# Average pooling over a contiguous input: the completion wait of two output stores moved behind the closing barriers, and the results moved from pool tiles to fixed SBUF tensors

## The chip, the cores and the metric

The kernel runs on one core of one Trainium2 chip. The metric is the device time of one execution in microseconds; the time before is the median of three runs. Beside these runs one execution was recorded by the hardware profiler; its rows are what the prediction works from. Engine names are those of the profile: DVE is VectorE, ACT is ScalarE, POOL is GpSimd, SP is SyncE, PE is TensorE. A "q" behind a name (SPq, POOLq) means the engine's sequencer, which issues DMAs and executes waits and barriers.

## What is computed

The input `x` has the shape (32, 256, 4096) in float32, 134.22 MB; `output_size` is 256. Each of the 32 x 256 = 8192 rows is cut into 256 windows of 16 neighbouring values, and the output (32, 256, 256) holds the mean of each window, 8.39 MB:

```python
for i in range(output_size):
    start = int(i * length / output_size)
    end = int((i + 1) * length / output_size)
    result[:, :, i] = np.mean(x[:, :, start:end], axis=-1)
```

## The kernel before

The 8192 rows are worked on in 16 tiles of 128 partitions x 4 rows: one tile is 128 x 16384 float32 values, 8.39 MB. The first fifteen tiles belong to one view of the input in which each partition owns 60 neighbouring rows (`x_many`), the last tile to a second view with 4 rows a partition (`x_last`). The one loop runs over the tiles `t`. In each turn

- SP issues the load of the tile into a buffer of `inpool` (L66). The pool has two buffers of 64 KiB a partition, so the load of tile t+2 waits until both reductions of tile t are done. In the last turn SP then issues the store of all fifteen earlier results, `o_many` from `res_many` (L68), in one DMA of 7.86 MB.
- POOL adds, for the second half of the tile's windows, the upper eight values of each window onto the lower eight, in place (L69).
- DVE sums the windows of the first half, sixteen values each (L74), and then those of the second half, eight values each (L77).
- ACT multiplies the tile's 1024 sums a partition by 1/16, in place (L80).

Behind the loop SP issues the second store, `o_last` from `res_last` (L85), 0.52 MB. Both stores wait for ACT. All DMAs of the kernel go through SP's one queue, in program order: sixteen loads, the large store, the small store.

The results lie in two tiles of a pool with one buffer each, `res_many` (60 KiB a partition) and `res_last` (4 KiB). The tile framework gives out the addresses and every semaphore. In bytes from the start of a partition, the two input buffers begin at 16,640 and 82,176 and the results at 147,712 and 209,152; a small tile `pad` that nothing reads or writes lies ahead of them and has the effect that all of them begin at a multiple of 256.

What follows the kernel's last instruction is written by the framework when its context closes; in the profile it carries the line of the `with` statement, L116. It is, in this order:

1. on SP, four waits for the eight DMA semaphores that loads and stores share (the third has the semaphore of the small store, the fourth that of the large one), then a drain that waits for ACT;
2. a barrier over all five engines: each reports to POOL, and POOL releases them;
3. on POOL, a drain and one instruction that clears the framework's semaphores, and a drain;
4. a second barrier of the same kind.

After that the runtime's own closing code runs, a barrier over the engines and the reset of all semaphores; it lies outside the profile's span.

Of the kernel before, what the change touches and what calls it, by code (L numbers as in the profile page):

```python
# [1 line left out]

# [4 lines left out]


@with_exitstack
def kernel(  # L10
    ctx: ExitStack,
    tc: tile.TileContext,
    x: bass.AP,
    output_size: int,
    out: bass.AP,
):

    nc = tc.nc
    F32 = mybir.dt.float32
    X = mybir.AxisListType.X

    batch, channels, length = x.shape
    ob, oc, olen = out.shape
    assert ob == batch and oc == channels and olen == output_size
    assert length % output_size == 0
    window = length // output_size  # L30
    hw = window // 2
    inv_w = 1.0 / float(window)

    P = nc.NUM_PARTITIONS
    R = 4
    rows = batch * channels
    assert rows % (P * R) == 0
    ntiles = rows // (P * R)
    many = (ntiles - 1) * R
    cells = R * output_size  # L40
    m = cells // 2
    cols = R * length

    xr = x.rearrange("b c l -> (b c) l")
    orow = out.rearrange("b c o -> (b c) o")
    x_many = xr[0 : P * many, :].rearrange("(p r) l -> p (r l)", p=P, r=many)
    o_many = orow[0 : P * many, :].rearrange("(p r) o -> p (r o)", p=P, r=many)
    x_last = xr[P * many :, :].rearrange("(p r) l -> p (r l)", p=P, r=R)
    o_last = orow[P * many :, :].rearrange("(p r) o -> p (r o)", p=P, r=R)

    padpool = ctx.enter_context(tc.tile_pool(name="padpool", bufs=1))
    padpool.tile([P, 32], F32, name="pad")
    inpool = ctx.enter_context(tc.tile_pool(name="inpool", bufs=2))
    respool = ctx.enter_context(tc.tile_pool(name="respool", bufs=1))
    res_many = respool.tile([P, (ntiles - 1) * cells], F32, name="res_many")
    res_last = respool.tile([P, cells], F32, name="res_last")

    for t in range(ntiles):
        last = t == ntiles - 1
        xin = inpool.tile([P, cells, window], F32, name="xin")  # L60
        if last:
            res, base, src = res_last, 0, x_last
        else:
            res, base = res_many, t * cells
            src = x_many[:, t * cols : (t + 1) * cols]
        nc.sync.dma_start(out=xin.rearrange("p o w -> p (o w)"), in_=src)  # L66
        if last:
            nc.sync.dma_start(out=o_many, in_=res_many[:, :])  # L68
        nc.gpsimd.tensor_add(  # L69
            out=xin[:, m:cells, 0:hw],  # L70
            in0=xin[:, m:cells, 0:hw],
            in1=xin[:, m:cells, hw:window],
        )
        nc.vector.reduce_sum(  # L74
            out=res[:, base : base + m], in_=xin[:, 0:m, :], axis=X
        )
        nc.vector.reduce_sum(  # L77
            out=res[:, base + m : base + cells], in_=xin[:, m:cells, 0:hw], axis=X
        )
        nc.scalar.mul(  # L80
            out=res[:, base : base + cells],
            in_=res[:, base : base + cells],
            mul=inv_w,
        )
    nc.sync.dma_start(out=o_last, in_=res_last[:, :])  # L85


# [1 line left out]
_INS = ['x', 'output_size']  # L89
_OUTS = [((32, 256, 256), 'float32')]  # L90

_NUMBERS = {'output_size': 256}


# [26 lines left out]
```

## Time and profile before

| | |
|---|---|
| median of 3 runs | 334.69 us (334.52 to 334.81) |
| the profiled execution | 335.07 us |
| its span, first to last instruction | 333.3 us |
| DMA engines, share of the span | 99.1 % (142.61 MB, 428 GB/s) |
| DVE busy | 209.7 us (63 %) |
| POOL busy | 139.7 us (42 %) |
| ACT busy | 18.2 us (5 %) |

The span runs from the first to the last instruction of the program; the profiled execution took 1.8 us more than its span. A busy share is an average over the whole span. Where times inside the span are given below, they count from its start. The trace also keeps each sequencer instruction and each update of a semaphore with its own time; where the text gives a time to the nanosecond it comes from there.

### The profile page before, as it was taken

To read this page: it belongs to the slowest core of one execution; us is meant where nothing else is said; L and a number is where in the kernel's file an instruction comes from. 1 tells how busy PE (TensorE), PEld (TensorE's weight loads), DVE (VectorE), ACT (ScalarE), POOL (GpSimd) and SP (SyncE) were. 2 spreads that over 40 slices of the span, in tenths; PEclk is the share of its full clock that TensorE was granted. 3 is DMA by queue.
4 is the path that set the end of the run, shared out by engine and by line. 5 is a ranking of instruction groups with operands and counts; after the bars stand their busy time and mean duration, and the time that the engine had idled before them with its cause. 6 is when DMAs were issued, how large, how long until landed. Compare 5 with 4: busy or idle time off the path is not lost.

```text
span 333.3 us, 158 instructions
## 1 busy us (share of the span) xinstructions
DVE 209.7 (63%) x32; ACT 18.2 (5%) x17; POOL 139.7 (42%) x20
## 2 busy tenths in 40 slices
DVE  0039295693929568392957849294774929487491
ACT  1000101000010100001010100101010010101001
POOL 0027090643709063360907346090724519082460
DMA  9898989999898989899898989899998989898996
GB/s 378 378 503 378 503 378 472 409 401 480 378 503 378 503 378 496 385 433 448 385 496 378 503 378 503 378 472 409 401 480 378 503 378 503 378 496 385 391 442 299
DMA packets 2592, 142.61 MB, mean 428 GB/s; under 512 B 288, under 2 KB 288, under 8 KB 416
## 3 DMA queue, kind: packets, MB, share of 16 engines
q1 hardware_dynamic: 2592, 142.61, 99.1%
HBM read 134.22 MB, written 8.39 MB: 428 GB/s over the span
## 4 chain that ended last, share of the span: by engine, by line
DMA 66%; POOL 18%; DVE 11%; POOLq 3%; issue 0%; ACT 0%; SPq 0%
DMA xin<-in_x_dram 66%; POOL xin L69 18%; DVE res_many L77 9%; POOLq L116 3%; DVE res_last L77 1%; ACT res_last L80 0%; SPq L66 0%; POOLq L69 0%
## 5 line engine op out<-in xcount | busy, mean ns | idle before, releaser
L69 POOL TENSOR_TENSOR xin<-xin 128x4096 f32<-128x4096 f32 x16 | 139.5, 8717 | 182.0 <-DMA xin<-in_x_dram 182.0
L74 DVE TENSOR_REDUCE res_many<-xin 128x512 f32<-128x8192 f32 x15 | 130.3, 8686 | 107.3 <-DMA xin<-in_x_dram 107.3
L77 DVE TENSOR_REDUCE res_many<-xin 128x512 f32<-128x4096 f32 x15 | 66.3, 4420 | 2.5 <-POOL xin L69 2.3
L80 ACT ACTIVATE res_many<-res_many 128x1024 f32<-128x1024 f32 x15 | 15.8, 1056 | 289.6 <-DVE res_many L77 289.6
L74 DVE TENSOR_REDUCE res_last<-xin 128x512 f32<-128x8192 f32 x1 | 8.7, 8685 | 6.7 <-DMA xin<-in_x_dram 6.7
L77 DVE TENSOR_REDUCE res_last<-xin 128x512 f32<-128x4096 f32 x1 | 4.4, 4420 | 0.2 <-POOL xin L69 0.2
L80 ACT ACTIVATE res_last<-res_last 128x1024 f32<-128x1024 f32 x1 | 1.1, 1056 | 18.9 <-DVE res_last L77 18.9
L80 ACT ACT_TABLE_LOAD x1 | 1.3, 1283 | 0.7 <-PEq L102 0.7
L102 POOL MEMSET const-float32-0.0<- 128x1 f32 x1 | 0.1, 98 | 0.2 <-issue 0.2
L102 POOL MEMSET const-bfloat16-1.0<- 128x1 bf16 x1 | 0.1, 101 | 0.0
L102 POOL MEMSET const-uint8-127<- 128x1 uint8 x1 | 0.1, 101 | 0.0
L102 POOL MEMSET const-float32-1.0<- 128x1 f32 x1 | 0.1, 98 | 0.0
## 6 DMA issues: line engine op xcount, KB each, us to landing
out_dram<-res_many SPq DMA_DIRECT2D x1, 7680.0 KB, 23.7
out_dram<-res_last SPq DMA_DIRECT2D x1, 512.0 KB, 4.9
xin<-in_x_dram SPq DMA_DIRECT2D x16, 25.3
```

Of the source, the lines that this page charges most:

```text
L69: nc.gpsimd.tensor_add(out=xin[:, m:cells, 0:hw], in0=xin[:, m:cells, 0:hw], in1=xin[:, m:cells, hw:window],)
L74: nc.vector.reduce_sum(out=res[:, base : base + m], in_=xin[:, 0:m, :], axis=X)
L77: nc.vector.reduce_sum(out=res[:, base + m : base + cells], in_=xin[:, m:cells, 0:hw], axis=X)
L80: nc.scalar.mul(out=res[:, base : base + cells], in_=res[:, base : base + cells], mul=inv_w,)
L102: nc = _bacc.Bacc("TRN2", target_bir_lowering=False, num_devices=1)
L116: with _tile.TileContext(nc) as tc:
```

## The change

- `res_many` and `res_last` are no longer pool tiles but SBUF tensors allocated at fixed places ahead of the pool, each aligned to 256 bytes; the unused `pad` tile goes. In the built program the results begin at 16,640 and 78,080 and the input buffers at 82,176 and 147,712.
- Both stores go through a helper `store`. It issues the same DMA on SP, keeps the framework from giving it a semaphore, and lets it add 16 to the kernel's own semaphore `stored` when it lands. The stores stand at the same places among SP's instructions as before and wait for ACT as before.
- At its end the kernel closes its pools and the framework's context itself, so that the closing code of the list above is written there. Behind it come two more things on SP: a wait until `stored` has reached 32, and the clearing of that semaphore. In the built program these are one instruction, a clear of one semaphore that carries the wait.

The order of instructions on DVE, ACT, POOL and PE is the same in both built programs.

```diff
-    padpool = ctx.enter_context(tc.tile_pool(name="padpool", bufs=1))
-    padpool.tile([P, 32], F32, name="pad")
+    res_many = nc.alloc_sbuf_tensor("res_many", [P, (ntiles - 1) * cells], F32, align_bytes=256)
+    res_last = nc.alloc_sbuf_tensor("res_last", [P, cells], F32, align_bytes=256)
     inpool = ctx.enter_context(tc.tile_pool(name="inpool", bufs=2))
-    respool = ctx.enter_context(tc.tile_pool(name="respool", bufs=1))
-    res_many = respool.tile([P, (ntiles - 1) * cells], F32, name="res_many")
-    res_last = respool.tile([P, cells], F32, name="res_last")
+
+    stored = nc.alloc_semaphore("stored")
+
+    def store(out, in_):
+        ins = nc.sync.dma_start(out=out, in_=in_)
+        tc.no_tile_sem_insts.add(ins.ins.name)
+        ins.then_inc(stored, 16)
...
         if last:
-            nc.sync.dma_start(out=o_many, in_=res_many[:, :])
+            store(o_many, res_many[:, :])
...
-    nc.sync.dma_start(out=o_last, in_=res_last[:, :])
+    store(o_last, res_last[:, :])
+
+    ctx.pop_all().close()
+    tc.close()
+    tc.compile()
+    nc.sync.wait_ge(stored, 32)
+    nc.sync.sem_clear(stored)
```

## The prediction

> **What bounds the kernel now.** I read the page first: the busy shares, the DMA row and the DMA queue.
>
> ```profile
> DVE 209.7 (63%) x32; ACT 18.2 (5%) x17; POOL 139.7 (42%) x20
> ...
> DMA  9898989999898989899898989899998989898996
> ...
> q1 hardware_dynamic: 2592, 142.61, 99.1%
> ```
>
> The reader is to see that no engine is near its limit and that the one queue of SP fills the sixteen DMA engines from end to end; only the last slice drops, to 6. A stretch-by-stretch view confirms it: four neighbouring tile periods, then the last load's work, ACT's last multiply, the flight of the small store, and what is left. Its columns are the length of the stretch, busy time by engine, the granted clock, the DMA share and GB/s.
>
> ```profile
> 99.26:118.60 19.34, 13.11 (x2) 1.06 (x1) 8.72 (x1) 1.00 1.00 434
> 118.60:137.95 19.35, 13.11 (x2) 1.06 (x1) 8.72 (x1) 1.00 1.01 437
> ...
> 326.40:327.46 1.06, 0.00 (x0) 1.05 (x1) 0.00 (x0) 1.00 0.00 0
> 327.46:332.30 4.84, 0.00 (x0) 0.00 (x0) 0.00 (x0) 1.00 0.73 311
> 332.30:333.30 1.00, 0.00 (x0) 0.00 (x0) 0.00 (x0) 1.00 0.00 0
> ```
>
> A tile takes 19.34 us of DMA against 13.11 us of DVE and 8.72 us of POOL, so compute waits for loads (a DMA row with 0.00 is a stretch in which no packet happened to begin: packets are 2.3 us long). The last line matters here: 1.00 us at the end in which nothing moves and no engine computes. Next the DMA issues, to place the landing of the last store, and the waits of SP's queue.
>
> ```profile
> out_dram<-res_many SPq DMA_DIRECT2D x1, 7680.0 KB, 23.7
> out_dram<-res_last SPq DMA_DIRECT2D x1, 512.0 KB, 4.9
> ...
> SPq L116 <- DMA out_dram<-res_last: 4.4, 1, 4.4
> SPq L116 <- PEq L116: 0.6, 2, 0.4
> ```
>
> The small store is issued at 327.48 and lands 4.9 us later, at 332.42 (the semaphore's sixteenth step stands at 332.417 in the trace). SP waits 4.4 us for it in the closing code. Only then come the two barriers, in which SP waits another 0.6 us. The rows of line 116 show what they are made of (duration in ns as min/median/max, then first and last start).
>
> ```profile
> L116 SPq EVENT_SEMAPHORE  x6: 17/28/4429, 327.9 to 333.2; - x6
> L116 POOLq EVENT_SEMAPHORE  x4: 17/17/17, 332.6 to 333.2; - x4
> L116 PEldq EVENT_SEMAPHORE  x2: 51/51/51, 332.8 to 333.2; - x2
> L116 POOLq EVENT_SEMAPHORE_RANGE_CLEAR  x1: 95/95/95, 332.9 to 332.9; - x1
> ```
>
> In order of time: landing 332.417; SP's wait ends 332.440; its remaining wait and two drains until 332.606; POOL releases everybody at 332.735; POOL clears the semaphores from 332.902 to 332.997; second gathering 333.105; second release, taken by SP at 333.225 to 333.242; PE's release ends last, at 333.287. That is 0.87 us from the landing to the end of the span, all of it serial.
>
> **The change, part by part.**
>
> *The barriers.* SP's last DMA issue ends at 327.82. Without the wait for the stores, SP's four waits find loads that landed before 313.1 and pass at 28 ns each; the drain finds ACT done at 327.45. The same rows that take from 332.476 (the first instruction behind the wait) to 333.287, 0.81 us, then run from about 328.0 to 328.8. That lies under the flight of the store, which ends at 332.42: 3.6 us of cover. If the store landed at once, the 0.81 us would be back on the path. The gather of the first barrier needs ACT, DVE and POOL; all have been done since 327.46. Cost on the path: nothing.
>
> *What remains behind the landing.* One clear with the wait in it, on SP. The trace has no such row on SP. The nearest is POOL's clear of eleven semaphores, 95 ns: its first semaphore falls 21 ns after its start and the eleventh 68 ns after, so a clear of one should take about 95 - 47 = 48 ns; 95 is the upper end. SP reacts 23 ns after the landing (332.417 to 332.440). So SP ends between 332.417 + 0.023 + 0.048 = 332.49 and 332.54; if the wait executes as an instruction of its own and the clear behind it, the steps of before (36 + 28 + 40 ns between them) make it 332.64. I take 332.52. SP leaves the program at 333.242 before, so it leaves 0.72 us earlier (0.60 to 0.75). The span, which ended with PE, shrinks by 333.29 - 332.52 = 0.77 to 332.52.
>
> *Behind the span.* 1.78 us of the profiled execution lie outside its span. In the trace the runtime's closing barrier follows: nine updates of one semaphore from 333.522 to 334.047, 0.525 us. The same nine updates ahead of the program take 0.371 us. The difference is one step of 205 ns where the opening barrier has 39: one engine came 0.166 us late. After the change four engines arrive 3.7 us early and only SP is late. If SP was that late engine, nothing more is gained (0). If it was another, the barrier goes as soon as SP does: at most, SP needs the 0.28 us until the first update (333.242 to 333.522) and half the steps behind it, 0.24, so 0.52 instead of 334.047 - 333.242 = 0.81, a gain of 0.29. SP's own waits in the rows above are among the shortest and PE's the longest, so I lean to another engine, but take 0.10, as I can't name it. The semaphore reset behind this barrier stays.
>
> The Trainium skill bears on this (Runtime: NRT & Kernel Launch, "The ~15µs preamble/postamble breakdown"): it books the closing barrier at about 1.5 us as a wait for all engines and describes the barrier itself as a hand-over from engine to engine with 44 ns a hop. Taken as a fixed 1.5 us it speaks against any gain outside the span, and the sum would be 0.72; the trace's 0.525 with one late hop leaves room for 0.82. The same table has the runtime reset the semaphores itself afterwards, which would make the added clear needless; it states no price for leaving it out.
>
> *The store's semaphore and the wait's place.* Both stores add 16 to `stored`, as many semaphore writes as before. SP issues nothing behind the wait and no engine of the program waits for SP there, so nothing queues behind it but SP's own exit. The stores keep their places behind the sixteenth load; the large one still waits for ACT's fifteenth multiply, the small one for the sixteenth. Zero.
>
> *The tensors' places.* `pad` issued no instruction. Loads and stores are as many and as large. The input buffers take the bases 82,176 and 147,712, the results 16,640; before, the buffers had 16,640 and 82,176 and the results 147,712. It is the same three regions, permuted. Loads into the two old buffers alternate from tile to tile, and the periods above are 19.34 and 19.35 us; in the trace a packet of 65,536 bytes takes 2418 ns into either (27.1 GB/s), and one of 61,440 bytes read from the third region takes 2267 ns (27.1 GB/s). So no region is slower than another in these rows. DVE's and POOL's rows (8.69, 4.42, 8.72 us) would have to grow by 6 us a tile before they held up a load. Zero, with the bound below as a rival.
>
> Sum: 0.72 + 0.10 = 0.82 us. The profiled execution would go from 335.07 to 334.25. It stood 0.38 us over the median of the runs; I carry that distance over: 334.69 - 0.82 = 333.87 us.
>
> **The rivals.**
>
> *The barriers do not hide* (nothing gained): the closing drain on SP waits for its DMAs in flight whatever the semaphores say, or the runtime's barrier takes back what the program's gave. For it: no row shows a drain on SP with a DMA under way. Against it: SP's three drains of 7 ns each come right after its waits and POOL's 8809 ns drain covers POOL's own addition only. Then the barriers stay behind the landing and the new instruction is added: 334.69 + 0.07 to 0.2, so 334.8.
>
> *The moved tensors slow the DMAs* (slower): if loads into the region at 147,712 ran slower than stores out of it, every second load would pay, and as the DMA queue is full, all of it would reach the end. Each engine moves 128 load packets; half of them go to that region. From 0.82 / 64 = 13 ns a packet (0.5 % of 2418) it eats the gain. At 2 % it costs 64 x 48 ns = 3.1 us: 334.69 - 0.82 + 3.1 = 337.0. For it: no load of before wrote to that region. Against it: DVE and ACT write there and the store reads there at the full 27.1 GB/s, and the two other regions do not differ.
>
> *The barrier of the runtime gives all it can* (faster still): 0.75 + 0.29 = 1.04, 333.65. It is the lower part of the forecast's own range.
>
> **How the numbers follow.** The forecast's case, with the gain between 0.60 and 1.04, gets 0.84; the rival without gain 0.09; the slower one 0.07. Three runs spread from 0.17 below to 0.12 above their median, so the range of the forecast reaches from 334.69 - 1.04 - 0.17 = 333.48 to 334.69 - 0.60 + 0.12 = 334.21; rounded outward to 333.4 and 334.3 it leaves out the two rivals, 0.16. About 0.2 % or 0.67 us is what a measurement of this kernel can tell from no change, and the forecast is close to that line: of its 0.84 I put 0.06 on gains too small to be told. Faster 0.78, within 0.2 % 0.06 + 0.09 = 0.15, slower 0.07.
>
> **What would show it.** Right: the last store is issued at 327.5 and lands at 332.4 as before; SP's rows of the closing code start right after the last issue and the barriers end before 329.5; the last instruction is SP's clear, shorter than 95 ns, within 0.15 us of the landing; the span is 332.5; tile periods stay at 19.34. Wrong: a long drain on SP; barrier rows behind 332.4; a landing that has moved (then the tensors' places count); a span that shrinks by 0.77 while the time does not, which would mean that the part outside the span has grown.

## The result, and the profile after

The changed kernel takes 333.52 us (median of 6 runs, 333.35 to 333.74), against 334.68 us before (334.52 to 335.13, 6 runs). The ratio is 0.9964 with a 95 % interval of 0.9951 to 0.9976: 1.16 us less. It lies in the predicted range and beyond the 0.82 us that were forecast. The profiled execution took 333.62 us over a span of 332.31 us; before it was 335.07 over 333.29. So the span gave 0.98 us and the part outside the span another 0.47.

The rows of the closing code, now line 93 (duration in ns as min/median/max, then first and last start in us):

```profile
L93 SPq EVENT_SEMAPHORE  x6: 17/28/28, 327.7 to 328.7; - x6
L93 POOLq EVENT_SEMAPHORE  x4: 17/17/17, 328.1 to 328.6; - x4
L93 SPq DRAIN  x3: 7/7/7, 328.0 to 328.3; - x3
L93 PEldq EVENT_SEMAPHORE  x2: 51/51/51, 328.2 to 328.7; - x2
L93 POOLq EVENT_SEMAPHORE_RANGE_CLEAR  x1: 95/95/95, 328.4 to 328.4; - x1
```

Everything that started at 332.5 to 333.2 before now starts at 327.9 to 328.7, close behind the last issue, which begins at 327.34 and ends at 327.69. Each of these rows has its old duration; only SP's longest wait has gone from 4429 ns to 28. SP's drains take 7 ns with a 0.52 MB store under way, so a drain on SP does not wait for the DMAs that SP issued here. The wait itself has moved to line 95:

```profile
L95 SPq EVENT_SEMAPHORE_RANGE_CLEAR  x1: 25/25/25, 332.3 to 332.3; - x1
```

In SP's waits, the landing is now awaited there; the barrier's 0.6 us are still in the list, but beside the store instead of behind it:

```profile
SPq L95 <- DMA out_dram<-res_last: 3.6, 1, 3.6
...
SPq L93 <- PEq L93: 0.6, 2, 0.4
```

The stretches of time, with the columns as before: two tile periods, ACT's last multiply, the flight of the small store, and what remains behind its landing.

```profile
99.30:118.60 19.30, 13.11 (x2) 1.06 (x1) 8.72 (x1) 1.00 1.00 435
118.60:138.00 19.40, 13.11 (x2) 1.06 (x1) 8.72 (x1) 1.00 1.01 436
326.26:327.34 1.08, 0.00 (x0) 1.05 (x1) 0.00 (x0) 1.00 0.00 0
327.34:332.27 4.93, 0.00 (x0) 0.00 (x0) 0.00 (x0) 1.00 0.72 306
332.27:332.31 0.04, 0.00 (x0) 0.00 (x0) 0.00 (x0) 1.00 0.00 0
```

The tile periods are what they were, and so is the flight of the last store, 4.94 us from issue to landing before and 4.93 after. The empty end has shrunk from 1.00 us (0.87 if it is counted from the landing) to 0.04. That leaves 0.15 us of the span's 0.98 that the closing code does not explain: the last landing stands at 332.268 instead of 332.417. The last load already landed 0.14 us earlier in this execution (312.920 instead of 313.061), and the store was issued 0.14 us earlier for it. Whether the moved tensors did that is the first thing to test.

The other 0.47 us lie behind the span, where the page has no rows, but the trace keeps the updates of the runtime's barrier semaphore. In us from the span's start, with the landing for comparison:

| | before | after |
|---|---|---|
| last landing | 332.417 | 332.268 |
| SP's last instruction ends | 333.242 | 332.310 |
| closing barrier, updates 1 to 4 | 333.522, .556, .761, .806 | 328.983, 329.017, .222, .266 |
| updates 5 to 9 | 333.829, .927, .966, 334.001, .047 | 332.432, .476, .514, .548, .596 |
| second barrier, first and sixth update | 334.833, 335.071 | 333.383, 333.621 |

Two things can be read here. The sixth update of the second barrier stands at 335.071 and 333.621, and the two executions took 335.07 and 333.62 us; in the eight executions profiled below it agrees with the time to 0.01 us as well. So the measured time is that from the first instruction to that update, and I can split it into the landing and a tail behind it: 335.071 - 332.417 = 2.654 us before and 333.621 - 332.268 = 1.353 us after. And four of the nine updates are made 3 us before SP arrives; when it does, its own update follows 0.122 us after its last instruction and the last one 0.164 us later.

### The profile page after: what moved, and what is told of

Same layout as the page of the kernel before. It is cut to its first block, busy times and chain, and to the rows that moved or that the text cites. A ratio compares the mean times of both kernels' runs of the same rounds, so it can differ in the third digit from the quotient of the medians.

```text
span 332.3 us, 159 instructions
## 1 busy us (share of the span) xinstructions
DVE 209.7 (63%) x32; ACT 18.2 (5%) x17; POOL 139.7 (42%) x20
## 4 chain that ended last, share of the span: by engine, by line
DMA 66%; POOL 18%; DVE 11%; POOLq 3%; issue 0%; ACT 0%; SPq 0%
DMA xin<-in_x_dram 66%; POOL xin L73 18%; DVE res_many L81 9%; POOLq L93 3%; DVE res_last L81 1%; ACT res_last L84 0%; SPq L70 0%; POOLq L73 0%
```

## The theories

A: all of the gain is the wait's place. It has two parts, the program's closing code, which now runs under the store's flight (0.825 - 0.042 = 0.78 us up to SP's last instruction), and the runtime's closing barrier, at which four engines have long arrived (the rest of 2.654 - 1.353 = 1.30, so 0.52 us). B: the new places of the tensors give part of it. C: the own semaphore gives it, whatever the place of the wait. D: the part outside the span is chance.

Each experiment below was timed against the kernel before on the same chip: the first four in one job (before 334.86 us, 27 runs), the other four in another (before 334.78 us, 14 runs).

## The parts one by one

**Only the fixed tensors.** All diffs from here on are against the changed kernel.

```diff
-    stored = nc.alloc_semaphore("stored")
-
-    def store(out, in_):
-        ins = nc.sync.dma_start(out=out, in_=in_)
-        tc.no_tile_sem_insts.add(ins.ins.name)
-        ins.then_inc(stored, 16)
-
...
-            store(o_many, res_many[:, :])
+            nc.sync.dma_start(out=o_many, in_=res_many[:, :])
...
-    store(o_last, res_last[:, :])
+    nc.sync.dma_start(out=o_last, in_=res_last[:, :])
 
-    ctx.pop_all().close()
-    tc.close()
-    tc.compile()
-    nc.sync.wait_ge(stored, 32)
-    nc.sync.sem_clear(stored)
```

> Only the fixed tensors; both stores keep the framework's semaphores and the closing code waits for them as before. Theory A (all of the gain is the wait's place): the last landing stays 0.87 us ahead of the span's end, 334.7 us, ratio 1.000 within 0.001. Theory B (the new places of buffers and results give part of it, since the last landing of the changed kernel came 0.15 us earlier): 334.4 to 334.5 us, with the last landing again at 332.27 us of the span.

Measured: 334.79 us (11 runs), ratio 0.9997 (0.9988 to 1.0005). The closing code, now line 114, stands behind the landing as before, and from the landing to the end of the span it is 0.870 us in both:

```profile
L114 SPq EVENT_SEMAPHORE  x6: 17/28/4417, 327.9 to 333.2; - x6
L114 POOLq EVENT_SEMAPHORE_RANGE_CLEAR  x1: 95/95/95, 332.9 to 332.9; - x1
```

The last landing is at 332.410, with the tensors in their new places, so 332.27 against 332.42 is no effect of them. The places neither gain nor lose anything that the runs can tell; theory B's 334.4 to 334.5 us is at the edge of the interval, and the next experiment is its second test.

**The wait last, with every buffer at its old address.** This kernel allocates the two input buffers as fixed tensors too, ahead of the results, which puts all four at the addresses of before.

```diff
+    xins = [
+        nc.alloc_sbuf_tensor(f"xin_{i}", [P, cells, window], F32, align_bytes=256)
+        for i in range(2)
+    ]
     res_many = nc.alloc_sbuf_tensor("res_many", [P, (ntiles - 1) * cells], F32, align_bytes=256)
     res_last = nc.alloc_sbuf_tensor("res_last", [P, cells], F32, align_bytes=256)
-    inpool = ctx.enter_context(tc.tile_pool(name="inpool", bufs=2))
...
-        xin = inpool.tile([P, cells, window], F32, name="xin")
+        xin = xins[t % 2][:, :, :]
```

> The wait comes last as in the changed kernel, but buffers and results lie at the very addresses of before (two input buffers as fixed tensors at 16,640 and 82,176, results at 147,712 and 209,152). Theory A: all of the gain, 333.5 us, ratio 0.9965 within 0.001. Theory B: 0.15 us to 0.3 us less of it, 333.7 to 333.8 us.

Measured: 333.61 us (5 runs), ratio 0.996 (0.9948 to 0.9973): the whole gain. The last landing is at 332.257, in the old places, and the tail behind it is 1.351 us, as in the changed kernel. B falls: new places with the old wait gain nothing, old places with the new wait gain all.

**The own semaphore, awaited ahead of the closing code.**

```diff
-    ctx.pop_all().close()
-    tc.close()
-    tc.compile()
     nc.sync.wait_ge(stored, 32)
-    nc.sync.sem_clear(stored)
```

> Fixed tensors and the kernel's own semaphore as in the changed kernel, but SP waits for it ahead of the closing code, so that the barriers stand behind the landing. Theory A: nothing gained, and as the four waits of 68 ns a step now all stand behind the landing where one did before, 0.2 us more than before: 334.9 us; landing to the end of the span 1.0 to 1.1 us. Theory C (the own semaphore itself is what is quicker, whatever its place): 333.5 to 334.0 us.

Measured: 335.18 us (11 runs), ratio 1.0011 (1.0002 to 1.002), slower by 0.32 us. The landing is awaited ahead of line 122's barriers (now by SP's branch into the closing code), and the waits and the clear of the closing code stand behind the landing at 331.92:

```profile
SPq L122 <- DMA out_dram<-res_last: 4.6, 1, 4.6
```

```profile
L122 SPq EVENT_SEMAPHORE  x6: 17/28/28, 332.1 to 333.1; - x6
...
L122 POOLq EVENT_SEMAPHORE_RANGE_CLEAR  x1: 95/95/95, 332.7 to 332.7; - x1
```

From the landing to the end of the span it is 1.21 us, 0.1 more than I expected: besides the four waits the branch too had to come behind the landing. The trace shows the whole loss there: the last of the four waits begins 0.391 us behind the landing, and 0.059 before, while from that wait to the end of the span it takes 0.82 us here and 0.81 before. C falls: without the place the own semaphore gains nothing.

## The part outside the span

**One more barrier behind the wait.** It brings the engines together again after the landing.

```diff
     nc.sync.sem_clear(stored)
+    nc.all_engine_barrier()
```

> The changed kernel with one more barrier over all five engines behind SP's wait. Theory A (two parts: some 0.78 us of program behind the landing, and some 0.5 us because four engines reach the runtime's closing barrier ahead of SP): the barrier costs its own 0.2 us on SP and also takes the second part back, since all engines leave the program together again; 0.7 us over the changed kernel, 334.1 to 334.3 us, and the time outside the span returns from 1.3 to about 1.8 us. Theory D (the part outside the span is chance): only the barrier's own 0.2 to 0.3 us, 333.7 to 333.8 us, outside the span 1.3 us.

Measured: 334.41 us (11 runs), ratio 0.9985 (0.9976 to 0.9994). The last store of the profiled execution lands at 332.037 and the span ends 0.302 us later; the last rows of line 96, which is the added barrier, show what happened:

```profile
L96 SPq DRAIN  x1: 7/7/7, 332.1 to 332.1; - x1
L96 SPq EVENT_SEMAPHORE  x1: 17/17/17, 332.3 to 332.3; - x1
...
L96 PEldq EVENT_SEMAPHORE  x1: 51/51/51, 332.3 to 332.3; - x1
```

The part outside the span is back at 1.79 us (before 1.78, changed kernel 1.31). The tail is 334.124 - 332.037 = 2.087 us, 0.73 more than the changed kernel's, where theory A had 0.7. The barrier's own instructions put SP's last end 0.21 us later behind the landing (0.256 instead of 0.042); the remaining 0.52 is the second part of theory A taken back. D falls.

**Who waits.** If the runtime's barrier is a chain in which every engine has its place, it must matter which engine comes last. Three kernels differ from the changed one only in the engine of the last two calls; shown is the one with POOL, the others have `nc.tensor` (PE) and `nc.scalar` (ACT):

```diff
-    nc.sync.wait_ge(stored, 32)
-    nc.sync.sem_clear(stored)
+    nc.gpsimd.wait_ge(stored, 32)
+    nc.gpsimd.sem_clear(stored)
```

> The changed kernel with the last wait and the clear on POOL instead of SP. In the runtime's closing barrier the third update comes 0.2 us after the second in both kernels, 0.56 us after POOL's last instruction. Theory A with POOL as that late engine: POOL's way out of 0.56 us and six updates of some 0.25 us stand behind the landing instead of SP's 0.12 and 0.16 us; 0.5 us over the changed kernel, 334.0 to 334.1 us, outside the span 1.8 us. Theory D (who waits is indifferent, or the part outside the span is chance): 333.5 us, outside the span 1.3 us.

> The changed kernel with the last wait and the clear on PE. Theory A with PE as the first of the runtime's barrier: way out 0.23 us, then all nine updates, 0.36 us, where SP had 0.12 and 0.16: 0.3 us over the changed kernel, 333.8 us, outside the span 1.6 us. If PE is not the first, between the changed kernel and the one that waits on POOL. Theory D: 333.5 us.

> The changed kernel with the last wait and the clear on ACT. Theory A with ACT as second in the runtime's barrier: eight updates, 0.32 us, behind its way out of 0.2 to 0.25 us: 0.25 to 0.3 us over the changed kernel, 333.8 us. Theory D: 333.5 us.

Measured: on POOL 334.00 us (8 runs, ratio 0.9975, 0.9965 to 0.9985), on PE 333.84 (6 runs, 0.9972, 0.9961 to 0.9984), on ACT 333.63 (6 runs, 0.9968, 0.9956 to 0.9980). The last instructions of the three, one line from each kernel:

```profile
L95 POOLq EVENT_SEMAPHORE_RANGE_CLEAR  x1: 44/44/44, 332.1 to 332.1; - x1
```

```profile
L95 PEldq EVENT_SEMAPHORE_RANGE_CLEAR  x1: 63/63/63, 332.3 to 332.3; - x1
```

```profile
L95 ACTq EVENT_SEMAPHORE_RANGE_CLEAR  x1: 41/41/41, 332.0 to 332.0; - x1
```

The span is then over within 0.1 us of the landing in each, so the spans alone would call the three equal. The updates of the closing barrier tell them apart, for the waiting engine leaves a gap of 3.2 to 3.8 us ahead of its update (with PE, which comes first, all nine updates stand behind the wait):

| who waits | updates made before it comes | its way out, last instruction to its update | from there to the ninth |
|---|---|---|---|
| PE | 0 | 0.239 us | 0.358 us |
| ACT | 1 | 0.119 us | 0.324 us |
| POOL | 2 | 0.527 us | 0.285 us |
| SP (changed kernel) | 4 | 0.122 us | 0.164 us |

So the order is PE, ACT, POOL, then by elimination DVE, then SP; whose the last four updates are, the traces do not say. And POOL's way out is four times that of SP. That is the late engine of the profile before: there POOL's last instruction ends at 333.200 and the third update follows at 333.761, 0.561 us later, after PE and ACT had reported at 333.522 and 333.556.

The wait on ACT came out 0.17 us quicker than the 333.8 us expected, because ACT's way out is 0.119 us and not 0.2 to 0.25. The waits on SP and ACT lie 0.18 us apart by the tail; as the first was not timed in the same job as the second, the times themselves don't separate them.

**Without the clear.**

```diff
     nc.sync.wait_ge(stored, 32)
-    nc.sync.sem_clear(stored)
```

> The changed kernel without the clear of the semaphore stored: SP ends with the bare wait. The clear took 25 ns in the trace, a wait 17 to 28 ns from its release. Theory A: no difference that can be measured, 333.5 us, the last instruction within 0.05 us of the landing. Rival (the clear is held back until its write has gone round): 0.05 to 0.1 us less.

Measured: 333.42 us (5 runs), ratio 0.9958 (0.9946 to 0.9971), last instruction 0.034 us behind the landing (17 ns of wait), tail 1.338 us instead of 1.353. That can't be told from the changed kernel, and the rival's 0.05 to 0.1 us is not there; the clear costs its 25 ns at most.

**All of it in one table.** Tail: from the last landing to the end of the time, one profiled execution each. The fourth column is the difference of the tails, the fifth that of the medians against the kernel before of the same job.

| kernel | landing, us | tail, us | tail against before | time against before |
|---|---|---|---|---|
| before | 332.417 | 2.654 | | |
| changed | 332.268 | 1.353 | -1.30 | -1.16 |
| only the fixed tensors | 332.410 | 2.654 | 0.00 | -0.07 |
| wait last, old places | 332.257 | 1.351 | -1.30 | -1.25 |
| wait ahead of the closing code | 331.918 | 2.990 | +0.34 | +0.32 |
| one more barrier | 332.037 | 2.087 | -0.57 | -0.45 |
| wait on POOL | 332.124 | 1.905 | -0.75 | -0.78 |
| wait on PE | 332.299 | 1.723 | -0.93 | -0.94 |
| wait on ACT | 331.962 | 1.533 | -1.12 | -1.15 |
| no clear | 331.862 | 1.338 | -1.32 | -1.36 |

The tails, read from a single trace each, give all nine differences of medians to within 0.14 us. The landings scatter over 0.56 us from execution to execution, and they are what spreads the runs: time less span is the same to 0.1 us in all runs of a kernel.

The two kernels without the own semaphore happen to have the latest landings of the table, which looks like one more effect of the change. It is none: the median less the tail puts their landings at 332.21 (before) and 332.14 us in the first job, and those of the three other kernels of that job at 332.19 to 332.32. The scatter arises ahead of the last store, for in all ten executions the last landing follows the last load's by 19.34 to 19.37 us. What moves the loads from run to run stays open.

## Why the prediction was right, and too small

- *The barriers hide under the store's flight*: right. They end at 328.75, 3.5 us before the landing, and no drain on SP waited. Predicted were 328.0 to 328.8.
- *What remains behind the landing*: 0.10 us forecast up to SP's last instruction, 0.042 measured. SP needs 17 ns to react instead of 23 and clears one semaphore in 25 ns instead of the 48 worked out from POOL's clear of eleven (POOL itself takes 44 for one). The term of 0.72 is 0.78.
- *Behind the span*: this is the term that was far too small. I gave it 0.10 us and at most 0.29; it is 0.52. The bound took the 0.28 us from SP's last instruction to the first update as time that SP needs. That update is PE's, and SP needs 0.122. It also took half of the steps behind the first update as SP's, without knowing SP's place; it is the fifth, with 0.164 us to go. The late engine was POOL: from 0.04 us ahead of SP's end, POOL's way out of 0.561 us and 0.286 us of updates behind it made 0.81 us; SP's 0.122 and 0.164 now make 0.29 in their place. A row of the trace had shown POOL's lateness as the 205 ns step, without a name. The prediction leaned away from SP because its waits were among the shortest and PE's the longest. Its conclusion, another engine than SP, was right, but by luck: those rows say nothing on how long an engine takes to leave the program.
- On the same step, the Trainium skill (Runtime: NRT & Kernel Launch, "The ~15µs preamble/postamble breakdown") describes the barrier as a hand-over with 44 ns a hop and books the closing one at about 1.5 us. The traces agree on the mean: where nobody is late, in the runtime's second barrier, the eight steps take 0.36 us, 45 ns each, though single ones take 23 to 99 ns. They do not show the 1.5 us: before the change the closing barrier took 0.53 us from its first to its ninth update, and 0.76 us from the program's last instruction. Read as a fixed cost the 1.5 us would have excluded the gain that was there. What counts is which engine comes last and how long its way out is.
- *The tensors' places, the semaphore's two times 16, the wait's place in SP's queue*: zero, as forecast; for the places the experiments with new places alone and old places alone show it, for the semaphore the one with its wait ahead of the closing code, where branch and waits make up the whole loss.
- *The three rivals*: the barriers that do not hide and the slower DMAs did not occur. The third, "The barrier of the runtime gives all it can", had the right sign, but its 333.65 us was still above the 333.52 measured. The largest gain that the prediction allowed was 1.04 us, and it was 1.16; the range held the time because it had been widened by the spread of the runs, so that part is luck.
- The 0.38 us by which the profiled execution of before stood over its median are landing, not tail (334.68 - 2.654 = 332.03 for the median run, 332.42 in the profile), so carrying them over was right. This takes the median run's tail to be that of the profile.

## What to carry to other kernels

Behind the last landing of an output stands not only what the program still executes but each engine's way out into the runtime's closing barrier; a last wait that sits on one engine alone, behind the program's own barriers, hides both for all the others, as long as they get there well ahead of it. Choose for it the engine with the shortest way out that comes latest in the chain: SP here, with 0.33 us from landing to the ninth update against 0.51 on ACT, 0.69 on PE and 0.88 on POOL (DVE was not tried). Where two kernels differ at the very end, split the time at the last landing: the tail repeats to some nanoseconds between traces of kernels that end alike (2.654 us twice, 1.353 and 1.351), while the landing scatters by tenths of a microsecond.

## What the runs showed of the hardware

- The measured time ends at the sixth update of the runtime's second closing barrier, to 0.01 us in all ten profiled executions; from the ninth update of the first closing barrier to that one it is 1.02 to 1.03 us in each.
- Engines leave a program at different speeds: from the last instruction to the report at the barrier 0.12 us on SP and ACT, 0.24 on PE, 0.53 to 0.56 on POOL.
- A clear of one semaphore takes 25 ns on SP, 41 on ACT, 44 on POOL and 63 on PE; of eleven on POOL 95.
- A drain on SP takes 7 ns while a store that SP issued is still under way.
